# An encoder layer on one core: the first shift-and-scale products run as one block, and one gate step moves ahead of the attention

## The chip, the core and the metric

The kernel runs on one core of a Trainium2 chip. A core has five engines with queues of their own: TensorE (PE in the profile; its weight loads are shown apart as PEld), VectorE (DVE), ScalarE (ACT), GpSimd (POOL) and SyncE (SP). All of SyncE's work here is to issue transfers from device memory to the on-chip memory SBUF. TensorE writes to PSUM, which has eight banks of 128 x 512 fp32 values. The metric is the device time of one execution in microseconds, the median over the runs.

## The reference

One layer of a bidirectional encoder is applied to two groups of 256 rows (prompt and sample) of width 1024, all in fp32:

```python
ada = silu(c) @ w_ada + b_ada
sh1, sc1, g1, sh2, sc2, g2 = split(ada, 6)
h = layernorm(x) * (1 + sc1) + sh1
rq, rk, rv, rg, dq, dkv, kr, gA, gB = split(h @ w_in)
# branch A: two-way retention over 4 heads with rq, rk, rv, gated by silu(rg), times w_ret_o -> y_a
# branch B: cq = rmsnorm(dq), ckv = rmsnorm(dkv); queries cq @ w_uq, keys ckv @ w_uk, values ckv @ w_uv,
#           a shared rotary key from kr; 8 heads of softmax attention, times w_mla_o -> y_b
f = (sigmoid(gA) * y_a + sigmoid(gB) * y_b) @ w_out
x = layernorm(alpha * x + (1 + g1) * f)
h = layernorm(x) * (1 + sc2) + sh2
# conv-gated MLP of width 2816 -> y
x = layernorm(alpha * x + (1 + g2) * y)
```

## The kernel before

The 512 rows of both groups stand side by side as columns: h is kept transposed as eight tiles `hT[k]` of 128 features x 512 rows, k = 0 to 7. Nearly every fp32 product is made of three TensorE matmuls (`mm3`, L161 to L163): each operand is split into a high part (a rounded cast, on ScalarE as a rule, L151) and a low part (the difference, on VectorE, L141), and high x high, high x low and low x high are added up in PSUM. A weight must therefore land, be cast and be subtracted before its second or third matmul can run. In the names `_r` is the raw weight, `_h` and `_l` are the parts.

The start works in four quarters q = 0 to 3, two h tiles each. `ada_sums(q)` (L371) multiplies silu(c) into eight pieces `wada` of 128 x 512, of which each product fills only 32 rows of a PSUM bank; four of them lie beside each other, so that the eight products of a quarter come in two rounds. `ada_rows` (L377) copies the sums to SBUF on ScalarE, `ada_done` turns them (TensorE, `ps_adx`, L384) and reduces them (VectorE, L386) to the shift `sh1` and scale `sc1` of the quarter; `h_tile` applies these to the turned, normalized x (`xT`, made by `flip_x`) and splits h. `latent(k)` adds h tile k times the latent weight `wlat` k (448 columns: dq, dkv, kr) into four banks `ps_lat`, and `gb_part` does the same for the first two tiles of gate B. `keep_warm` (L291) issues matmuls of ones whose result is not used.

Before, quarter 0's products are cut in two: four stand inside the first turned tile, four behind the fourth, and each later quarter's two fours have latent products between them. `lat_hi` casts the first latent weight on ScalarE; its low part (`lat_lo`) is handed to `h_tile` and made on VectorE between the two halves of h tile 0.

After the last latent product come the norms and the latent rows: `latent_rows` turns the latents, scales them and splits them to `cqT0`, `cqT1` and `ckvT`. The rest of gate B and the first piece of gate A lie in a row of steps, `fill_b` (32 steps of six matmuls, 128 x 512). `take(fill_b, cost)` draws steps until the cost is reached, 1.3 for each; ahead of the attention `take(fill_b, 2.6)` draws two. A weight of a gate is loaded and split once for eight steps. The attention (`mla`) is a generator that yields a cost with each piece, and `interleave` draws a gate step whenever the gates' cost falls behind a fixed share, so the places of the steps in the attention are set by costs alone. While a head pair is worked on, the next pair's projections are made: `mla_proj(j)` splits weight `wm` j and makes `qn`, `kn`, `qr` and `v`; `scores` makes `ps_s`, its negative maximum `nm` and the exponentials `p`; `flip` turns `p`.

TensorE's order is the order of the program throughout. ScalarE's and VectorE's orders are that of the program in the start (up to the last `gb_part`), and from there a scheduler of the language sets them at build time. SyncE issues the loads in the order of the program as their buffers come free; raw weights, high parts and low parts have two buffers each.

Of the kernel before, what the change touches and what calls it, by code (L numbers as in the profile page):

```python
# [22 lines left out]

NP = 7

WARM_FIRST, WARM_THEN, WARM_FLIP = 9, 16, {1: 5, 3: 2}
IN_ORDER = {PE, mybir.EngineType.Activation, mybir.EngineType.DVE}

D = 1024
# [2 lines left out]
NK = D // 128  # L32
# [5 lines left out]
LATENT = 448  # L38
# [71 lines left out]
def encoder_kernel(ctx: ExitStack, tc: tile.TileContext, ins, outs):  # L110
# [264 lines left out]
    def ada_rows(q):  # L375
        ada_rows_of[q] = t512(F32, f"row{q}")
        act.copy(ada_rows_of[q], ps_ada.pop(q))  # L377
# [35 lines left out]
    def flip_x(k):  # L413
        ps = ps512(f"ps_xt{k}")
        for t in range(4):
            if k == 0 and t == 2:
                ada_sums(0, range(4))
            elif k == 0 and t:
                keep_warm(WARM_FLIP[t])
            pe.transpose(ps[:, t * 128:(t + 1) * 128], xs[t][k // 4][:, (k % 4) * 128:(k % 4) * 128 + 128], ident)  # L420
        xT[k] = t512(F32, f"xT{k}")
        (dve.tensor_copy if k in (1, 3) else act.copy)(xT[k], ps)
# [6 lines left out]

    lat_parts = {}  # L430

    def lat_hi(k):
        wl = lat_parts[k] = tuple(w[:, :LATENT] for w in (t512(F32R, f"wlat{k}_h"), t512(F32R, f"wlat{k}_l")))
        act.copy(wl[0], lat_raw[k][:, :LATENT])

    def lat_lo(k):
        wl = lat_parts[k]
        sub(wl[1], lat_raw.pop(k)[:, :LATENT], as32(wl[0]))

    def lat_split(k):  # L440
        lat_hi(k)
        lat_lo(k)

    def latent(k, ts=range(4)):
# [33 lines left out]
    def ada_chunk(which, cc):  # L478

        col = which * D + cc * 512  # L480
        acc = [t512(F32, f"acc{which}_{cc}_{g}") for g in range(2)]
        for kq in range(4):
            for k in range(2):
                raw = t512(F32, f"araw{which}_{cc}_{kq}_{k}")
                nc.sync.dma_start(raw, w_ada[:, kq * 2 + k, col:col + 512])
                for g in range(2):
                    s = csil[:, g, kq * 2 + k:kq * 2 + k + 1]
                    if kq == 0 and k == 0:
                        dve.tensor_scalar(out=acc[g], in0=raw, scalar1=s, scalar2=None, op0=ALU.mult)
                    else:  # L490
                        dve.scalar_tensor_tensor(out=acc[g], in0=raw, scalar=s, in1=acc[g],  # L491
                                                 op0=ALU.mult, op1=ALU.add)
            yield 0.0
        parts = [split(acc[g], f"accp{which}_{cc}_{g}") for g in range(2)]
        if which in (2, 5):
            bb = t512(F32, f"bb{which}_{cc}")
            nc.gpsimd.dma_start(bb, ins["b_ada"][:, col:col + 512].to_broadcast([128, 512]))
        yield 0.0
        yield 0.0
        for g in range(2):  # L500
            ps = ps512(f"ps_sum{which}_{cc}_{g}")
            pe.matmul(ps, ones, parts[g][0], start=True, stop=False)
            pe.matmul(ps, ones, parts[g][1], start=False, stop=True)
            full = t512(F32, f"ada{which}_{cc}_{g}")
            if which in (2, 5):
                dve.scalar_tensor_tensor(out=full, in0=ps, scalar=1.0, in1=bb, op0=ALU.add, op1=ALU.add)
                if which == 5:
                    act.mul(full, full, 1.0 / ALPHA)
                gates[which, g, cc] = full
            else:  # L510
                blocks = full.rearrange("p (k f) -> p k f", k=4)
                mul(blocks, ps.rearrange("p (k f) -> p k f", k=4), ident.unsqueeze(1).to_broadcast([128, 4, 128]))
                v = small(4, f"adv{which}_{cc}_{g}")
                dve.reduce_sum(out=v, in_=blocks, axis=AX.X)
                dst, one = (sh2, 0.0) if which == 3 else (sc2, 1.0)
                ks = slice(cc * 4, cc * 4 + 4)
                dve.scalar_tensor_tensor(out=dst[:, ks, g], in0=v, scalar=one, in1=bT[:, which, ks], op0=ALU.add, op1=ALU.add)
        yield 0.86


    with tc.manual_schedule(engines={PE}):
# [67 lines left out]
        with tc.manual_schedule(engines=IN_ORDER - {PE}):  # L589
            start_b()  # L590
            norm_x()
            flip_x(0)
            flip_x(1)
            flip_x(2)
            flip_x(3)
            ada_sums(0, range(4, NK))
            ada_rows(0)
            lat_hi(0)
            ada_done(0)
            h_tile(0, lambda: lat_lo(0))  # L600
            lat_hi(1)
            h_tile(1, lambda: lat_lo(1))
            flip_x(4)
# [1 line left out]
            load_vectors()  # L605
            latent(0, (2, 3, 0, 1))
            latent(1, (2, 3))
            ada_sums(1, range(4))
            latent(1, (0, 1))
            gb_split(0)  # L610
            lat_split(2)
            ada_sums(1, range(4, NK))
            ada_rows(1)
            gb_part(0, (0,))
            for q in range(1, 4):
                if q > 1:
                    latent(2 * q - 2)
                    lat_split(2 * q)
                    ada_sums(q, range(4))
                    latent(2 * q - 1, range(2))  # L620
                    ada_sums(q, range(4, NK))
                    ada_rows(q)
                    latent(2 * q - 1, range(2, 4))
                ada_done(q)
                h_tile(2 * q)
                lat_split(2 * q + 1)
# [61 lines left out]
        act.copy(K2[64:128], ps[0:64])  # L688
        sub(KL[0][0:64], ps[0:64], as32(K2[0:64]))
        act.copy(KL[1][64:128], as32(KL[0][0:64]))  # L690
        take(fill_b, 2.6)


        w_uq = ins["w_uq"][0].rearrange("(k p) (h f) -> p k h f", p=128, f=192)
# [727 lines left out]
```

## Time and profile before

| | us |
|---|---|
| Median of 3 runs (lowest, highest) | 864.46 (864.42, 866.68) |
| The profiled execution | 865.91 |
| Its span, with a granted TensorE clock of 0.997 | 864.1 |
| TensorE busy | 849.4 |
| VectorE busy | 612.1 |
| ScalarE busy | 379.1 |
| GpSimd busy | 95.0 |

The span runs from the first to the last recorded event, and the time of the execution lies 1.8 us above it. The start with its quarters takes the span's first 52 us, norms and latent rows come up to about 76, the attention up to 175, and then come the output of branch B, retention, merge and the MLP. A row of the timeline gives start, duration, engine, line, operation, output<-inputs, and in brackets the engine's idle time ahead of it with what ended it. A TensorE matmul's duration includes the time until its result is out, so consecutive matmuls overlap in these rows, and the distance of their starts is what one costs.

### The profile page before, as it was taken

What the parts mean: (1) busy time and instruction counts of PE and PEld (TensorE: products, weight loads), DVE (VectorE), ACT (ScalarE), POOL (GpSimd) and SP (SyncE); (2) the same over time, 40 slices, a digit from 0 to 9 for tenths busy, and PEclk for the clock granted to TensorE, in tenths of its full rate; (3) what the DMA queues carried; (4) which work ended last, traced back from release to release, by engine and by line L of the source; (5) the groups of instructions that cost most, each with busy time, mean ns of one, the idle gap of its engine ahead of it and who ended that gap; (6) DMA issues with size and microseconds to landing.
All of it is one profiled execution on the core that took longest, in us unless ns stands there. A gap on an engine that the chain in (4) does not pass through costs nothing.

```text
span 864.1 us, 11309 instructions
## 1 busy us (share of the span) xinstructions
PE 849.4 (98%) x4209; PEld 710.7 (82%) x4209; DVE 612.1 (71%) x1052; ACT 379.1 (44%) x647; POOL 95.0 (11%) x141
## 2 busy tenths in 40 slices
PE   8999999999999999999999999999999999999996
PEld 5678888988878888888888899888888888888885
DVE  5465888883687788796977867578657756855666
ACT  3564877551344344354343265334433535443500
POOL 3031012363000101000010200000000000100100
PEclk9999999999999999999999999999999999999998
DMA  9943156799465533553358323255343564655731
GB/s 296 352 151 110 50 154 182 197 295 240 146 179 175 171 114 118 156 181 138 117 159 261 121 87 98 74 157 156 97 138 121 154 176 133 157 166 150 263 115 66
DMA packets 129624, 137.63 MB, mean 159 GB/s; under 512 B 8757, under 2 KB 96403, under 8 KB 129568
## 3 DMA queue, kind: packets, MB, share of 16 engines
q1 hardware_dynamic: 118864, 112.75, 41.8%
q0 software_dynamic: 9888, 23.14, 11.7%
q10 hardware_dynamic: 816, 1.02, 0.3%
q8 instruction: 33, 0.54, 0.2%
q14 instruction: 23, 0.19, 0.1%
HBM read 129.53 MB, written 22.03 MB: 175 GB/s over the span
## 4 chain that ended last, share of the span: by engine, by line
PE 91%; DVE 3%; DMA 2%; ACT 2%; issue 1%; SPq 0%; ACTq 0%; DVEq 0%
PE ps_b L161 5%; PE ps_b L163 5%; PE ps_b L162 5%; PE ps_a L162 5%; PE ps_a L163 5%; PE ps_a L161 5%; PE ps_d L163 4%; PE ps_d L162 4%; PE ps_d L161 4%; PE ps_ga L161 2%; PE ps_ga L162 2%; PE ps_ga L163 2%; PE ps_rg L162 2%; PE ps_rg L163 2%; PE ps_ya L163 2%; PE ps_rg L161 2%
## 5 line engine op out<-in xcount | busy, mean ns | idle before, releaser
L491 DVE SCALAR_TENSOR_TENSOR acc<-araw,csil,acc 128x512 f32<-128x512 f32 x112 | 77.9, 748 | 18.8 <-DMA araw<-in_w_ada_dram 18.8
L161 PE MATMUL ps_b<-h_h,wup_h 128*128 128x512 f32 (+1 forms) x200 | 72.8, 364 | 0.3 <-ACT h2m L401 0.3
L162 PE MATMUL ps_a<-h_l,wup_h 128*128 128x512 f32 (+1 forms) x200 | 72.9, 365 | 0.1
L163 PE MATMUL ps_a<-h_h,wup_l 128*128 128x512 f32 (+1 forms) x200 | 72.8, 364 | 0.0
L161 PE MATMUL ps_a<-h_h,wup_h 128*128 128x512 f32 (+1 forms) x200 | 72.8, 364 | 0.0
L163 PE MATMUL ps_b<-h_h,wup_l 128*128 128x512 f32 (+1 forms) x200 | 72.7, 364 | 0.0
L162 PE MATMUL ps_b<-h_l,wup_h 128*128 128x512 f32 (+1 forms) x200 | 72.7, 364 | 0.0
L141 DVE TENSOR_TENSOR wup_l<-wup_r,wup_h 128x1024 fp32r<-128x1024 f32 (+1 forms) x46 | 52.7, 1173 | 8.4 <-ACT wup_h L151 7.7
L151 ACT CAST wup_h<-wup_r 128x1024 fp32r<-128x1024 f32 (+1 forms) x46 | 44.3, 1013 | 27.8 <-PE ps_b L162 20.0
L144 DVE TENSOR_TENSOR conv<-conv,ps_b 128x512 f32<-128x512 f32 x22 | 15.1, 686 | 40.2 <-PE ps_b L163 36.7
L161 PEld LDWEIGHTS ps_b<-h_h,wup_h 128*128 128x128 f32 x200 | 37.7, 189 | 6.4 <-ACT h2m L401 0.5
L162 PEld LDWEIGHTS ps_a<-h_l,wup_h 128*128 128x128 f32 x200 | 37.7, 189 | 6.3 <-DVE h_l L141 0.3
L163 PEld LDWEIGHTS ps_a<-h_h,wup_l 128*128 128x128 f32 x200 | 37.7, 189 | 6.2 <-DVE wup_l L141 0.2
L162 PEld LDWEIGHTS ps_b<-h_l,wup_h 128*128 128x128 f32 x200 | 37.7, 189 | 6.0
L163 PEld LDWEIGHTS ps_b<-h_h,wup_l 128*128 128x128 f32 x200 | 37.7, 189 | 5.9
L161 PEld LDWEIGHTS ps_a<-h_h,wup_h 128*128 128x128 f32 x200 | 37.7, 189 | 5.8
L1203 ACT ACTIVATE conv<-ps_a,vecs 128x512 f32<-128x512 f32 x22 | 17.2, 780 | 41.7 <-PE ps_a L163 41.7
L1205 DVE SCALAR_TENSOR_TENSOR conv<-ps_a,vecs,conv 128x510 f32<-128x510 f32 x22 | 16.4, 747 | 24.0 <-ACT conv L1203 24.0
L1209 ACT ACTIVATE conv<-conv 128x512 f32<-128x512 f32 x22 | 13.9, 633 | 41.2 <-DVE conv L1207 41.1
L1274 POOL DMA_DIRECT2D x1d<-ux x12 | 10.7, 929 | 175.9 <-DVE ux L144 111.4
L848 POOL DMA_DIRECT2D wsum<-in_w_down_dram x42 | 28.1, 1171 | 7.3 <-DMA wsum<-in_w_down_dram 7.1
L151 ACT CAST w_h<-w_r 128x1024 fp32r<-128x1024 f32 (+1 forms) x20 | 17.9, 944 | 19.2 <-PE ps_d L163 10.2
(383 smaller groups left out, 2461.6 us busy)
## 6 DMA issues: line engine op xcount, KB each, us to landing
wup_r<-in_w_up_dram SPq DMA_DIRECT2D x44, 512.0 KB, 5.3
araw<-in_w_ada_dram SPq DMA_DIRECT2D x64, 256.0 KB, 5.6
wsum<-in_w_down_dram POOLq DMA_DIRECT2D x42, 256.0 KB, 7.7
wada<-in_w_ada_dram SPq DMA_DIRECT2D x32, 256.0 KB, 5.9
w_r<-wsum SPq DMA_DIRECT2D x28, 256.0 KB, 3.8
wga_r<-in_w_in_dram SPq DMA_DIRECT2D x4, 1024.0 KB, 5.4
wmo_r<-in_w_mla_o_dram SPq DMA_DIRECT2D x4, 1024.0 KB, 5.3
wqk_r<-in_w_in_dram SPq DMA_DIRECT2D x8, 512.0 KB, 5.5
```

Source lines behind the costliest of these rows:

```text
L141: return (eng or dve).tensor_tensor(out=out, in0=a, in1=b, op=ALU.subtract)
L144: (eng or dve).tensor_tensor(out=out, in0=a, in1=b, op=ALU.mult)
L151: last_split.append(act.copy(hi, src).ins)
L161: pe.matmul(out, l[0], r[0], start=start, stop=False, skip_group_check=skip)
L162: pe.matmul(out, l[0], r[1], start=False, stop=False, skip_group_check=skip)
L163: pe.matmul(out, l[1], r[0], start=False, stop=stop, skip_group_check=skip)
L491: dve.scalar_tensor_tensor(out=acc[g], in0=raw, scalar=s, in1=acc[g], op0=ALU.mult, op1=ALU.add)
L848: tc.keep_in_program_order(nc.gpsimd.dma_start(dst, src, **kw))
L1203: act.activation(a, pa, AF.Identity, scale=convw[:, 1, f:f + 1], bias=convb[:, f:f + 1])
L1205: dve.scalar_tensor_tensor(out=av_[:, :, 1:256], in0=pv[:, :, 0:255], scalar=convw[:, 0, f:f + 1], in1=av_[:, :, 1:256], op0=ALU.mult, op1 ...
L1209: act.activation(a, a, AF.Gelu)
L1274: nc.gpsimd.dma_start(x1_rows(t, c), u, accum_op=ALU.add)
```

## The change

In quarter 0 all eight shift-and-scale products now stand together behind the second turned tile, the third and fourth tile are turned behind them, and matmuls of ones stand at the place of the four that left (`WARM_FLIP` has 3 for the place t = 2). The first latent weight is split whole ahead of the sums' copy, with the cast on VectorE in place of ScalarE. In each later quarter the eight products stand together: in quarter 1 behind all latent products, in quarters 2 and 3 behind one row tile's latent products of the odd h tile. One more gate step is drawn ahead of the attention (3.9 in place of 2.6, three steps). The edit in `ada_chunk` only writes the same two matmuls as a loop.

```diff
-WARM_FIRST, WARM_THEN, WARM_FLIP = 9, 16, {1: 5, 3: 2}
+WARM_FIRST, WARM_THEN, WARM_FLIP = 9, 16, {1: 5, 2: 3, 3: 2}
...
     def flip_x(k):
         ps = ps512(f"ps_xt{k}")
         for t in range(4):
-            if k == 0 and t == 2:
-                ada_sums(0, range(4))
-            elif k == 0 and t:
+            if k == 0 and t:
                 keep_warm(WARM_FLIP[t])
...
-    def lat_hi(k):
+    def lat_hi(k, eng=None):
         wl = lat_parts[k] = tuple(w[:, :LATENT] for w in (t512(F32R, f"wlat{k}_h"), t512(F32R, f"wlat{k}_l")))
-        act.copy(wl[0], lat_raw[k][:, :LATENT])
+        (eng.tensor_copy if eng else act.copy)(wl[0], lat_raw[k][:, :LATENT])
...
-    def lat_split(k):
-        lat_hi(k)
+    def lat_split(k, eng=None):
+        lat_hi(k, eng)
         lat_lo(k)
...
             flip_x(0)
             flip_x(1)
+            ada_sums(0)
+            lat_split(0, dve)
+            ada_rows(0)
             flip_x(2)
             flip_x(3)
-            ada_sums(0, range(4, NK))
-            ada_rows(0)
-            lat_hi(0)
             ada_done(0)
-            h_tile(0, lambda: lat_lo(0))
+            h_tile(0)
...
             latent(1, (2, 3))
-            ada_sums(1, range(4))
             latent(1, (0, 1))
             gb_split(0)
             lat_split(2)
-            ada_sums(1, range(4, NK))
+            ada_sums(1)
             ada_rows(1)
...
                     lat_split(2 * q)
-                    ada_sums(q, range(4))
-                    latent(2 * q - 1, range(2))
-                    ada_sums(q, range(4, NK))
+                    latent(2 * q - 1, range(1))
+                    ada_sums(q)
                     ada_rows(q)
-                    latent(2 * q - 1, range(2, 4))
+                    latent(2 * q - 1, range(1, 4))
...
-        take(fill_b, 2.6)
+        take(fill_b, 3.9)
```

Three places show how instructions move. The first is VectorE's queue at the start, before: `xT` are copies of turned tiles, `adv0` the reduction for shift and scale of quarter 0, `h0_l` and `wlat0_l` low parts.

```order
L422 COPY xT1_329<-ps_xt1_324 128x512
L422 COPY xT3_343<-ps_xt3_338 128x512
L386 TENSOR_REDUCE adv0_359<-ps_adx0_354 128x8
L147 TENSOR_TENSOR sh1_236<-adv0_359,bT_197 128x4
L389 SCALAR_TENSOR_TENSOR sc1_237<-adv0_359,bT_197 128x4
L405 TENSOR_SCALAR hm0_1_365<-xT0_322,sc1_237,sh1_236 128x256
L141 TENSOR_TENSOR h0_l_364<-hm0_1_365,h0_h_363 128x256
L141 TENSOR_TENSOR wlat0_l_352<-wlat0_115,wlat0_h_351 128x448
```

The same queue with the change:

```order
L420 COPY xT1_327<-ps_xt1_322 128x512
L432 CAST wlat0_h_338<-wlat0_115 128x448
L141 TENSOR_TENSOR wlat0_l_339<-wlat0_115,wlat0_h_338 128x448
L420 COPY xT3_356<-ps_xt3_351 128x512
L386 TENSOR_REDUCE adv0_363<-ps_adx0_358 128x8
L147 TENSOR_TENSOR sh1_236<-adv0_363,bT_197 128x4
```

The first latent weight's cast, new on this engine, and its low part now stand ahead of the copy of the fourth tile, and so ahead of the reduction.

The second place is TensorE in quarter 2, before, from the last latent product of h tile 2 on (h tiles 2 and 3 are worked on while the shifts of quarter 2 are summed).

```order
L163 MATMUL ps_lat3_241<-wlat2_h_440,h2_l_463 128x448
L371 MATMUL ps_ada2_525<-wada2_0_146,c32_195 32x512
L371 MATMUL ps_ada2_525<-wada2_1_148,c32_195 32x512
L371 MATMUL ps_ada2_525<-wada2_2_150,c32_195 32x512
L371 MATMUL ps_ada2_525<-wada2_3_152,c32_195 32x512
L161 MATMUL ps_lat0_238<-wlat3_h_472,h3_h_476 128x448
...
L163 MATMUL ps_lat1_239<-wlat3_h_472,h3_l_477 128x448
L371 MATMUL ps_ada2_525<-wada2_4_154,c32_195 32x512
```

With the change:

```order
L163 MATMUL ps_lat0_238<-wlat3_h_475,h3_l_480 128x448
L371 MATMUL ps_ada2_531<-wada2_0_146,c32_195 32x512
L371 MATMUL ps_ada2_531<-wada2_1_148,c32_195 32x512
L371 MATMUL ps_ada2_531<-wada2_2_150,c32_195 32x512
L371 MATMUL ps_ada2_531<-wada2_3_152,c32_195 32x512
L371 MATMUL ps_ada2_531<-wada2_4_154,c32_195 32x512
L371 MATMUL ps_ada2_531<-wada2_5_156,c32_195 32x512
L371 MATMUL ps_ada2_531<-wada2_6_158,c32_195 32x512
L371 MATMUL ps_ada2_531<-wada2_7_160,c32_195 32x512
L161 MATMUL ps_lat1_239<-wlat3_h_475,h3_h_479 128x448
```

The two fours have become one block, one latent group (three matmuls) later than the first four stood and one group earlier than the last four.

The third place is VectorE in the attention, about the second head pair's projections (`qn1_1`, `kn1_1`, `v1_0`, `v1_1`), the next pair's weight `wm2` and the fourth gate weight `wgb3`. Before:

```order
L141 TENSOR_TENSOR qn1_1_l_1191<-ps_qn1_1_1183,qn1_1_h_1190 128x512
L769 TENSOR_REDUCE nm1_0_1230<-ps_s1_0_1219 128x2
L141 TENSOR_TENSOR kn1_1_l_1199<-ps_kn1_1_1194,kn1_1_h_1198 128x512
L141 TENSOR_TENSOR v1_0_l_1210<-ps_v1_0_1202,v1_0_h_1209 128x512
L141 TENSOR_TENSOR wm2_l_1330<-wm2_r_1322,wm2_h_1329 128x640 x2
L776 RECIPROCAL r1_0_1236<-sm1_0_1233 128x2
L769 TENSOR_REDUCE nm1_1_1271<-ps_s1_1_1260 128x2
L141 TENSOR_TENSOR v1_1_l_1248<-ps_v1_1_1240,v1_1_h_1247 128x512
L778 TENSOR_SCALAR p1_0_1232<-p1_0_1232,r1_0_1236 128x256 x2
L141 TENSOR_TENSOR wgb3_l_1351<-wgb3_r_1348,wgb3_h_1350 128x1024 x2
```

With the change:

```order
L141 TENSOR_TENSOR qn1_1_l_1200<-ps_qn1_1_1192,qn1_1_h_1199 128x512
L765 TENSOR_REDUCE nm1_0_1239<-ps_s1_0_1228 128x2
L141 TENSOR_TENSOR wgb3_l_1295<-wgb3_r_1292,wgb3_h_1294 128x1024 x2
L141 TENSOR_TENSOR kn1_1_l_1208<-ps_kn1_1_1203,kn1_1_h_1207 128x512
L141 TENSOR_TENSOR wm2_l_1350<-wm2_r_1342,wm2_h_1349 128x640 x2
L141 TENSOR_TENSOR v1_0_l_1219<-ps_v1_0_1211,v1_0_h_1218 128x512
L772 RECIPROCAL r1_0_1245<-sm1_0_1242 128x2
L765 TENSOR_REDUCE nm1_1_1280<-ps_s1_1_1269 128x2
L141 TENSOR_TENSOR v1_1_l_1257<-ps_v1_1_1249,v1_1_h_1256 128x512
```

The split of `wgb3`, which stood behind all of these, now stands ahead of `kn1_1_l`, and that of `wm2` ahead of `v1_0_l`. ScalarE's casts of the same four moved in the same way.

More of the change, by code (lines that the diff above doesn't have):

```diff
@@ L501, in ada_chunk @@
             ps = ps512(f"ps_sum{which}_{cc}_{g}")
-            pe.matmul(ps, ones, parts[g][0], start=True, stop=False)
-            pe.matmul(ps, ones, parts[g][1], start=False, stop=True)
+            for part in parts[g]:
+                pe.matmul(ps, ones, part, start=part is parts[g][0], stop=part is parts[g][1])
             full = t512(F32, f"ada{which}_{cc}_{g}")
```

## The prediction

> **What bounds the kernel now.** I read the chain of waits first, then the busy time by stage, then the start and the attention as a timeline.
>
> ```profile
> span 864.1 us, 11309 instructions
> PE 91%; DVE 3%; DMA 2%; ACT 2%; issue 1%; SPq 0%; ACTq 0%; DVEq 0%
> ...
> 18.30:22.30 4.00, 2.32 (x18) 1.53 (x14) 1.91 (x7) 2.72 (x6) 0.00 (x0) 1.00 1.10 348
> ...
> 22.30:51.80 29.50, 29.50 (x164) 20.23 (x164) 14.14 (x33) 14.32 (x27) 4.50 (x3) 1.00 1.02 332
> ...
> 88.20:175.10 86.90, 86.56 (x550) 77.56 (x549) 71.94 (x143) 63.48 (x147) 18.50 (x32) 1.00 0.56 155
> 175.10:864.10 689.00, 679.71 (x3247) 571.50 (x3246) 489.39 (x779) 271.69 (x415) 58.21 (x80) 1.00 0.52 152
> ```
>
> The columns of the stage rows are length, then busy time of PE, PEld, DVE, ACT and POOL with counts, granted clock, DMA share and GB/s. TensorE carries 91% of the chain and is busy for 86.56 of 86.90 us in the attention (88.2 to 175.1): what is won before it arrives at the end unless the attention gives some back. After 175.1 the change alters no tensor work, so I let the gain or loss at 175 stand for the whole. Only small gaps can be won. The matmuls between 22.3 and 51.8 show as busy throughout, yet a matmul's shown time includes its drain, so I read start times there, not busy time. The DMA engines are full until 51.8 (share 1.0 to 1.1), so landings there depend on bytes queued, not on what TensorE does.
>
> **The start (take −0.56).** The gap ends in the latent products.
>
> ```profile
> 17.50 1.07 PE L371 MATMUL ps_ada<-wada,c 128*32 128x512 f32 x8
> ...
> 19.84 1.04 PE L420 MATMUL ps_xt<-cst,x 128*128 128x128 f32 x8
> 20.04 0.19 DVE L386 TENSOR_REDUCE adv<-ps_adx 128x8 f32<-128x32 f32 x1 [1.74 <-PE ps_adx L384]
> ...
> 21.25 0.47 PE L161 MATMUL ps_lat<-wlat_h,h_h 128*128 128x448 f32 x1 [0.38 <-ACT h_h L404]
> 21.57 0.62 DVE L141 TENSOR_TENSOR wlat_l<-wlat,wlat_h 128x448 fp32r<-128x448 f32 x1
> 22.25 0.48 PE L162 MATMUL ps_lat<-wlat_l,h_h 128*128 128x448 f32 x1 [0.52 <-DVE wlat_l L141]
> 22.56 0.36 PE L163 MATMUL ps_lat<-wlat_h,h_l 128*128 128x448 f32 x1
> ...
> 23.48 0.62 DVE L141 TENSOR_TENSOR wlat_l<-wlat,wlat_h 128x448 fp32r<-128x448 f32 x1
> ...
> 25.65 0.37 PE L163 MATMUL ps_lat<-wlat_h,h_l 128*128 128x448 f32 x1
> ```
> ```profile
> 10.65 1.05 SPq L229 DMA_DIRECT2D wada<-in_w_ada_dram  x2
> ...
> wada<-in_w_ada_dram SPq DMA_DIRECT2D x2, 256.0 KB, 5.9
> ...
> 24.58 7.19 SPq L229 DMA_DIRECT2D wada<-in_w_ada_dram  x8
> ...
> wada<-in_w_ada_dram SPq DMA_DIRECT2D x2, 256.0 KB, 5.8
> ```
>
> The second latent matmul waits for the low part of the first latent weight: 22.25 where a follower comes 0.31 after its predecessor (22.25 to 22.56, with an exposed weight load). From the third (22.56) to the eighteenth (25.65) are 15 steps of 0.206. Without the wait the third would start at 21.25+0.31+0.21 = 21.77 instead of 22.56: 0.79. The change makes that low part on VectorE before the shift and scale are ready. Its new cast waits there for the weight: the last shift-and-scale piece of quarter 0 is issued at 11.70−0.37 = 11.33 and lands 5.9 later, at 17.2; the latent weight is next in the same queue and lands within the next microsecond, by 18.0 (my estimate from 256 KB pieces at 349 GB/s). Cast and subtraction, 0.62 each at most, end by about 19.2.
>
> The eight shift-and-scale products now run in one run from about 15.35 and cannot end before the piece of 17.2. Four products take 1.07 us; what is left for the last piece ends near 18.3, against 17.50+1.07 = 18.57 before. But two transposed tiles (8 transposes, 1 us by the row of 19.84) now stand behind them, ahead of the row's turning, and VectorE copies one of them (about 0.7, as its work on 128x512 out of PSUM takes below) ahead of the reduction: about 19.2+0.05+0.7 = 20.0 against the reduction's 20.04. The first latent matmul therefore stays at 21.25; I cost the re-ordering itself at nothing, with −0.2 to +0.6 as bounds (the upper one if cast and subtraction run 0.6 later than said and hold the copy up).
>
> Part of the 0.79 returns. The next latent weight's low part is still made at 23.48 to 24.10, behind h on VectorE, and the fourteenth matmul, which needs it, would now come at 21.77+11×0.206 = 24.04. With 0.06 for the release (21.57+0.62 to 22.25) and an exposed load of 0.1 that costs up to 0.23. So −0.79+0.23 = **−0.56**, between 0 and −0.79.
>
> **Eight products together (take −0.28, −0.10, −0.28).**
>
> ```profile
> 25.94 1.06 PE L371 MATMUL ps_ada<-wada,c 128*32 128x512 f32 x8
> 26.94 0.47 PE L161 MATMUL ps_lat<-wlat_h,h_h 128*128 128x448 f32 x1
> 27.25 0.36 PE L162 MATMUL ps_lat<-wlat_l,h_h 128*128 128x448 f32 x1
> ...
> L371 PE MATMUL ps_ada<-wada,c x48: 592/605/617, 12.7 to 39.1; 128*32 128x512 f32 x48
> ...
> 35.89 0.37 PE L163 MATMUL ps_lat<-wlat_h,h_l 128*128 128x448 f32 x1
> ```
>
> A group of four starts 25.94−(25.65+0.206) = 0.085 late, holds the next load for 1.00 (26.94) and leaves a slow first follower (0.31 where 0.206 is usual: 0.10). Inside, 1.06 less one matmul's 0.605 is 0.455: two passes of that, and 0.09 until the load. Two groups cost 2×(0.085+0.91+0.09+0.10) = 2.37; eight together 0.085+1.82+0.09+0.10 = 2.10. Saved: about **0.28** in each of three quarters, bounds 0 and −0.35.
>
> Quarter 2 gives some back. Its last piece is issued at 24.58+7.19−0.37 = 31.40 and lands 5.8 later, at 37.2. The gain so far (0.84) puts the end of the first four latents at 35.89+0.21−0.84 = 35.26, three more take 0.62, and the eight begin at 35.96. The fifth to eighth piece are wanted after two passes, at 36.87, so the eighth is 0.35 late. What of this reaches the end depends on how the last passes overlap: 0 to 0.35, I take 0.18. In quarters 1 and 3 I assume all pieces have landed.
>
> **One more gate step before the attention (take −0.76).**
>
> ```profile
> 76.40 0.39 PE L161 MATMUL ps_qn<-cqT_h,wm_h 128*128 128x512 f32 x1
> ...
> 77.09 0.40 PE L161 MATMUL ps_qn<-cqT_h,wm_h 128*128 128x512 f32 x1
> 77.24 0.69 DVE L141 TENSOR_TENSOR cqT_l<-cqT_f,cqT_h 128x512 fp32r<-128x512 f32 x1
> ...
> 77.98 0.50 PE L162 MATMUL ps_qn<-cqT_l,wm_h 128*128 128x512 f32 x1 [0.49 <-DVE cqT_l L141]
> 78.31 0.39 PE L163 MATMUL ps_qn<-cqT_h,wm_l 128*128 128x512 f32 x1
> ```
>
> Three matmuls take 77.09−76.40 = 0.69, or 0.23 each. The one due at 77.32 starts at 77.98 (0.66), and its follower comes 0.33 later instead of 0.23: 0.76. A gate step is six such matmuls, 1.38, and now stands ahead of these; the same work falls out later, so it costs nothing by itself. At the new place cqT_l (77.93) is wanted at 78.70: the whole **0.76** goes, bounds −0.6 and −0.8.
>
> **What the step moves in the attention (take +1.06).** Gates are computed in a fixed row of steps; one taken early brings each later gate weight's split one slot forward. The split of the fourth gate weight thereby comes, on ScalarE and VectorE, ahead of three splits that the attention needs at once.
>
> ```profile
> 103.78 0.68 DVE L769 TENSOR_REDUCE nm<-ps_s 128x2 f32<-128x512 f32 x1
> 104.38 0.68 DVE L141 TENSOR_TENSOR kn_l<-ps_kn,kn_h 128x512 fp32r<-128x512 f32 x1
> 104.97 0.69 DVE L141 TENSOR_TENSOR v_l<-ps_v,v_h 128x512 fp32r<-128x512 f32 x1
> 105.57 1.55 DVE L141 TENSOR_TENSOR wm_l<-wm_r,wm_h 128x640 fp32r<-128x640 f32 x2
> ...
> 108.82 2.36 DVE L141 TENSOR_TENSOR wgb_l<-wgb_r,wgb_h 128x1024 fp32r<-128x1024 f32 x2
> 111.09 0.70 DVE L141 TENSOR_TENSOR pT_l<-ps_pt,pT_h 128x512 fp32r<-128x512 f32 x1
> ...
> 102.78 0.61 ACT L151 CAST kn_h<-ps_kn 128x512 fp32r<-128x512 f32 x1
> ...
> 106.76 2.00 ACT L151 CAST wgb_h<-wgb_r 128x1024 fp32r<-128x1024 f32 x2
> ...
> 108.41 0.40 PE L161 MATMUL ps_qn<-cqT_h,wm_h 128*128 128x512 f32 x1
> ```
>
> In before, the second head's kn_l and v_l come straight behind nm, then wm_l, and wgb_l long after. In the change nm is followed by wgb_l, kn_l, wm_l, v_l. Starts on VectorE lie closer than the shown times: 0.59 behind 0.68 (104.38 to 104.97), 2.27 behind 2.36 (108.82 to 111.09), so about 1.47 behind 1.55. On before's axis: wgb_l at 104.38 (its casts, 2.00 us on ScalarE, take the place of kn_h at 102.78 and end at 104.8, ahead of its second half's start at about 105.5), kn_l at 106.65, wm_l at 107.25, v_l at 108.72, done at 109.41. The next head's qn matmuls, which by the program wait for that v_l to free their bank, cannot start before 109.47. Before they start at 108.41: **+1.06**. The earlier wait for kn_l and scores is inside this. Bounds: 0, if the bank is free earlier than I read, and +1.39 with full times in a row (103.78+0.68+2.36+0.68+1.55+0.69 = 109.74). I take 1.06, since these rows show the overlap.
>
> **Sum.** −0.56−0.28−0.10−0.28−0.76+1.06 = −0.92. The profiled execution took 865.91 with a span of 864.1; it becomes 864.99. It lies 1.45 over the median of the runs, 864.46, which moves by the same amount, to **863.5**. A difference below 0.3% (2.6 us, to 861.87 or 867.05) can hardly be told from none.
>
> **Rivals.**
> First, no wait in the attention: other banks come round, or TensorE has slack there that I missed. For it: in the stage 88.2 to 175.1 TensorE is short of busy by only 0.34, so before all splits came in time. Against it: VectorE is busy 71.94 of 86.90, and 2.27 of work enters ahead of an operand. Then −1.98: 862.5.
>
> Second, slower: the moved splits hold VectorE up twice, in full. At the fourth gate weight 1.39, and one slot early again at the first of the other gate's weights, whose split of the same shape (2.36) then stands ahead of the reduction for a softmax. Together 3.75, more than the 1.98 won elsewhere, from which point it decides: +1.8, 866.2. Against it: there only the reduction is passed, and a split's own halves leave room.
>
> Third, the start brings nothing: VectorE's early cast waits for its weight and delays the copy, reduction and h by 0.6, which eats the 0.56; TensorE then comes late enough in quarter 2 to find its last piece landed. Then 0−0.28×3−0.76+1.06 = −0.54: 863.9. For it: the bound of +0.6 above. Against it: the landing of the latent weight by 18.0 leaves cast and subtraction the time in which TensorE transposes.
>
> Fourth, the clock falls. From 15.3 on TensorE now has eight products, of which the last wait for their pieces until 17.2, and then a thinly filled stretch until 21.25.
>
> ```profile
> 1.48 4.21 PE L291 MATMUL ps_warm<-ones 128*128 128x512 f32 x9 [1.48 <-DVE ones L276]
> ```
>
> A cold start shows its price: nine matmuls in 4.21, 0.47 each against 0.23 at speed, so about 2.1 lost. Net −0.92+2.1 = +1.2: 865.6. Against it: granted clock is 1.00 between 18.3 and 22.3, where TensorE is busy 2.32 of 4.00. The Trainium skill (TensorE: Matmul & The Clock Gate, section "What's actually happening") says that an idle window of about 3.4 us halves the clock. By that rule the gaps here, each under 2 us, would not close it, and the row of 18.3 to 22.3 agrees.
>
> **How the numbers follow.** The forecast gets 0.50, the first rival 0.20, the second 0.12, the third 0.12, the fourth 0.06. The forecast's own bounds are 863.1 (0.23 and 0.18 not given back: −1.33) to 864.4 (nothing from the start, 1.39 in the attention: −0.92+0.56+0.33 = −0.03). The range 862.2 to 865.1 takes in the first and third rival, and of the second as much as half of its second place (1.39+1.18−1.98 = +0.6); it leaves out the rest of the second and the fourth. Only the second or fourth with more on top passes 867.05, and only more gain than any term shows passes 861.87: faster 0.06, same 0.89, slower 0.05.
>
> **What would show it.** Right: first latent near 21.2 and the second 0.31 behind it; one run of eight products per quarter, with no latent between them; in quarter 2 a DMA wait inside the group; no wait for cqT_l; in the attention TensorE waits near 105 to 108 (on the new axis) for kn_l and v_l, with wgb_l ahead of both. Wrong: the first latent later than 21.5, TensorE waits anywhere after 110, or a granted clock under 1 at 18 to 22. A total gain near 2 us would say that the attention's queue did not matter; a loss, that it mattered twice.

## The result and the profile after

The change made the kernel slower: 870.86 us in the median (869.38 to 872.24), against 865.33 for the kernel before (864.42 to 870.2) in 11 runs each. The ratio is 1.0054, with an interval of 1.004 to 1.0068. The forecast was 863.5. The profiled execution of the change took 869.88 with a span of 868.1, which is 4.0 over the 864.1 of before.

The chain of waits of the change, and its busy time by stage, on the stages that were shown of before (but the first begins at 17.50 in place of 18.30, and the last ends at the new span):

```profile
PE 91%; DMA 3%; DVE 3%; ACT 1%; issue 1%; SPq 0%; DVEq 0%; ACTq 0%
...
17.50:22.30 4.80, 4.27 (x29) 3.36 (x28) 3.39 (x10) 3.21 (x7) 0.00 (x0) 1.00 1.10 349
22.30:51.80 29.50, 29.50 (x169) 21.33 (x168) 15.04 (x37) 15.16 (x29) 4.75 (x3) 1.00 1.01 331
...
88.20:175.10 86.90, 86.25 (x542) 76.87 (x541) 72.07 (x142) 64.55 (x148) 19.29 (x33) 1.00 0.53 137
175.10:868.10 693.00, 678.58 (x3238) 571.10 (x3236) 487.15 (x777) 268.21 (x412) 55.99 (x78) 0.99 0.52 153
```

The last stage is 4.0 longer than before while TensorE's busy time in it is 1.1 shorter: the loss is idle time behind 175.1, in the stage that the prediction took as untouched. Between 170 and 260 the waits of TensorE name one place:

```profile
PE ps_yb L163 <- DVE wmo_l L141: 5.3, 1, 5.3
```

`ps_yb` is branch B's output, with four weights `wmo0` to `wmo3` in turn; each is loaded, cast and subtracted like the others. The timeline of the change around that wait, TensorE first, then VectorE, then SyncE:

```profile
194.94 0.39 PE L162 MATMUL ps_yb<-attn_l,wmo_h 128*128 128x512 f32 x1
200.66 0.80 PE L163 MATMUL ps_yb<-attn_h,wmo_l 128*128 128x512 f32 x1 [5.33 <-DVE wmo_l L141]
201.25 0.63 PE L161 MATMUL ps_yb<-attn_h,wmo_h 128*128 128x512 f32 x1
...
203.69 0.40 PE L161 MATMUL ps_yb<-attn_h,wmo_h 128*128 128x512 f32 x1
...
194.74 1.41 DVE L489 SCALAR_TENSOR_TENSOR acc<-araw,csil,acc 128x512 f32<-128x512 f32 x2 [15.38 <-DMA araw<-in_w_ada_dram]
...
199.39 1.22 DVE L141 TENSOR_TENSOR wmo_l<-wmo_r,wmo_h 128x1024 fp32r<-128x1024 f32 x1
...
164.26 0.34 SPq L483 DMA_DIRECT2D araw<-in_w_ada_dram  x1
174.94 0.37 SPq L192 DMA_DIRECT2D wmo_r<-in_w_mla_o_dram  x1
175.36 11.52 SPq L483 DMA_DIRECT2D araw<-in_w_ada_dram  x7
...
DMA to landing us min/median/max: 5.9/20.2/21.5
```

The last row is from the view of the `araw` tiles between 160 and 200. The same two queues before:

```profile
165.10 4.79 SPq L485 DMA_DIRECT2D araw<-in_w_ada_dram  x8
178.61 0.38 SPq L192 DMA_DIRECT2D wmo_r<-in_w_mla_o_dram  x1
...
DMA to landing us min/median/max: 6.8/7.3/7.6
```

`araw` are pieces of the weight for the second layer half's shift, scale and gates; VectorE multiplies them by silu(c) and adds them up (`ada_chunk`), in a long side work that only fills gaps. Before, all eight pieces of the first chunk were issued from 165.10 on, landed in 7 us, and the load of `wmo3` came behind them at 178.61. In the change the order that is made at build time puts the load of `wmo3` ahead of seven of them. (Unlike what the description of the kernel says, SyncE's order too is made at build time: in the program four of these pieces stand ahead of the load of `wmo1`, while in the trace of before the loads of `wmo1` and `wmo2` come ahead of all eight, at 145.32 and 153.32.) That load waits for a raw buffer, which comes free when `wmo1` is subtracted, at 174.9; SyncE issues in order, so the seven pieces left from 175.36 on, over 11.5 us, and took 20 us in the median. VectorE also works in order: it stood 15.38 us in front of the late piece, with the low part of `wmo2` behind it. TensorE lost 200.66−194.94−0.23 = 5.5 there. Then the seven intervals to 203.69 took 3.03 where seven at 0.23 take 1.6: 1.4 more.

How far the change was ahead (−) or behind at one and the same matmul is read from the two timelines. Each row is one execution. The first column is that execution's own start. It ranges over 2.2 us, and the latest starts are those in which the matmuls of ones at the beginning ran slowly:

```profile
7.52 3.92 PE L291 MATMUL ps_warm<-ones 128*128 128x512 f32 x16
7.49 6.71 PE L295 MATMUL ps_warm<-ones 128*128 128x512 f32 x16
```

The first row is of before, the second of skip_slot5_sum_later: there twelve of the fifteen distances between starts are 0.43 us, where in before all but the first are 0.23 or 0.24. Eight of the 13 traces, but not those of before and the change, have six or more distances of 0.43.

| Start in the kernel's trace minus that of before, us | first latent (21.25) | last latent (60.79) | first ps_yb (175.16) | last ps_yb (219.40) | last ps_rg (367.29) |
|---|---|---|---|---|---|
| the change | −0.37 | −2.03 | −2.23 | +4.74 | +3.87 |
| two_steps | −0.45 | −1.53 | −1.54 | −1.54 | +0.19 |
| step_alone | +1.34 | +1.28 | +1.06 | +8.67 | +7.66 |
| load_behind | −0.80 | −1.81 | −1.98 | −1.95 | +1.14 |
| third_raw_buffer | −0.82 | −2.29 | −2.48 | +13.66 | +12.66 |
| wmo2_low_on_gpsimd | −0.54 | −2.21 | −2.40 | −2.11 | +1.54 |
| start_alone | −0.42 | −1.02 | −1.04 | −1.04 | −2.04 |
| two_steps_sum_later | −0.50 | −2.17 | −2.17 | −2.17 | −2.49 |
| load_behind_sum_later | +0.12 | −1.52 | −1.69 | −1.66 | −1.90 |
| skip_slot5 | −0.26 | −1.88 | −2.10 | −2.10 | −2.47 |
| skip_slot5_sum_later | +0.86 | −0.81 | −1.03 | −1.03 | +0.75 |
| skip_slot6_sum_later | +0.37 | −1.29 | −1.50 | −1.50 | −2.13 |

From 367 to the end no kernel's shift changes by more than 0.15. The kernel before ran from 863.7 to 872.4 over all the runs here, so the ratios, each against runs of before on the same chip, have wide intervals, and the traces carry more than they do.

### The profile page after: what moved, and what is told of

Same layout as the page of the kernel before. It is cut to its first block, busy times and chain, and to the rows that moved or that the text cites. A ratio compares the mean times of both kernels' runs of the same rounds, so it can differ in the third digit from the quotient of the medians.

```text
span 868.1 us, 11318 instructions
## 1 busy us (share of the span) xinstructions
PE 849.6 (98%) x4212; PEld 713.2 (82%) x4212; DVE 612.3 (71%) x1053; ACT 378.1 (44%) x646; POOL 93.6 (11%) x141
## 3 DMA queue, kind: packets, MB, share of 16 engines
q10 hardware_dynamic: 816, 1.02, 0.3%
## 4 chain that ended last, share of the span: by engine, by line
PE 91%; DMA 3%; DVE 3%; ACT 1%; issue 1%; SPq 0%; DVEq 0%; ACTq 0%
PE ps_b L161 5%; PE ps_b L162 5%; PE ps_b L163 5%; PE ps_a L162 5%; PE ps_a L163 5%; PE ps_a L161 5%; PE ps_d L162 4%; PE ps_d L161 4%; PE ps_d L163 4%; DMA araw<-in_w_ada_dram 2%; PE ps_ga L161 2%; PE ps_ga L162 2%; PE ps_rqk L161 2%; PE ps_rg L161 2%; PE ps_rqk L162 2%; PE ps_rv L161 2%
## 5 line engine op out<-in xcount | busy, mean ns | idle before, releaser
L163 PE MATMUL ps_yb<-attn_h,wmo_l 128*128 128x512 f32 x64 | 25.7, 401 | 5.3 <-DVE wmo_l L141 5.3
```

The costliest lines, as they stand in the source:

```text
L163: pe.matmul(out, l[1], r[0], start=False, stop=stop, skip_group_check=skip)
```

## The experiments

### Which part of the change does it: two_steps, step_alone

The first undoes one part, the second does it alone on the kernel before.

```diff
 two_steps (on the change)
-        take(fill_b, 3.9)
+        take(fill_b, 2.6)
 step_alone (on the kernel before)
-        take(fill_b, 2.6)
+        take(fill_b, 3.9)
```

> The change with two gate steps ahead of the attention, as before, and the rest of the change kept. Theory A: the loss comes from the third gate step alone. It shifts the build-time order so that the load of the last output weight of branch B (wmo3) stands ahead of seven araw loads and holds them; VectorE then waits for araw with wmo2's low part behind it. Without the step that order is as before: no wait of TensorE for wmo_l, cqT_l waited for again (about 0.7), span about 2.0 under before (862.1, from the shift of 2.0 that the change shows at the end of quarter 3). Theory B: the loss comes from reaching the output of branch B earlier, when its weights have not landed; then at least 2 of the 5.3 us of waiting remain and the span is 864 or more.

> The kernel before with three gate steps in place of two and nothing else. Theory A: the same late araw loads and a wait of TensorE for wmo_l of 4 to 6 us; the time some 5 us over before (won 0.8 at cqT_l, 0.6 behind it, lost 1.2 in the attention, 6.9 at the output of branch B, 0.9 regained behind it). Theory B: TensorE gets there at before's time within 1 us, so no such wait, and the time is within 1 us of before.

Measured: two_steps 864.66 (ratio 0.999, interval 0.9972 to 1.0009, span 864.3); step_alone 871.87 (ratio 1.007, 1.0044 to 1.0096, span 871.7). In two_steps the wait at `ps_yb` is gone, and 1.54 of lead stands at 219.40. In step_alone it is there, with none of the new start. TensorE's wait and SyncE's queue in step_alone:

```profile
PE ps_yb L163 <- DVE wmo_l L141: 5.6, 1, 5.6
...
167.55 0.34 SPq L485 DMA_DIRECT2D araw<-in_w_ada_dram  x1
178.24 0.37 SPq L192 DMA_DIRECT2D wmo_r<-in_w_mla_o_dram  x1
178.66 11.73 SPq L485 DMA_DIRECT2D araw<-in_w_ada_dram  x7
```

So the gate step alone makes the late loads, and Theory B (coming too early) falls: step_alone reached branch B's output 1.06 later than before and still waited. But two_steps did not keep its lead: span 864.3 where 862.1 was expected. It lost 1.7 at another place, between 219 and 254:

```profile
252.60 0.50 PE L501 MATMUL ps_sum<-accp_h,ones 128*128 128x512 f32 x1 [1.71 <-ACT accp_h L151]
```

These matmuls sum the second chunk of the side work. Before, they start at 252.41, so their operand came 0.2 later although all ahead of them was 1.5 sooner.

### Is it SyncE's order: load_behind, third_raw_buffer

```diff
 load_behind (on the change)
-        for dst, src in pieces(raw):
-            nc.sync.dma_start(dst, src)
+        with tc.issue_after(last_piece[0]) if name == "wmo3" else nullcontext():
+            for dst, src in pieces(raw):
+                nc.sync.dma_start(dst, src)
...
+                if which == 4 and cc == 0:
+                    last_piece[:] = [d.ins]
 third_raw_buffer (on the change)
-    T_BUFS = 72
+    T_BUFS = 68
-        raw = wpool.tile([128, 2048], F32, tag="raw", name=name + "_r", bufs=2)
+        raw = wpool.tile([128, 2048], F32, tag="raw", name=name + "_r", bufs=3)
```

> The change with one edit: the load of wmo3 is kept behind the last of the eight araw loads in SyncE's queue. Theory A: araw lands in about 7 us as before, no wait for wmo_l; the shift of the change at the start of branch B's output (0.85 us ahead of before, with the gate step counted) stands to the end: span 863.0 to 863.5. Theory B: a wait of several us stays, since the weights themselves are what is late; span over 866.

> The change with three buffers for raw weights in place of two (four of the 72 general tiles given up for it). The load of wmo3 stands ahead of all araw loads in SyncE's queue but waits for no buffer any more. Theory A1: the harm of the order is that SyncE stands still until wmo1's buffer comes free; then araw is issued near 165, lands within about 10 us, and TensorE waits less than 1 us for wmo_l: span 863 to 865. Theory A2: the harm is that 1 MB goes ahead of araw in the transfer; then araw lands 10 us or more later than in before and the wait for wmo_l stays at 3 us or more.

Measured: load_behind 864.92 (ratio 0.999, 0.9967 to 1.0013, span 865.2). SyncE's queue is as before again, and there is no wait at `ps_yb`:

```profile
164.52 4.62 SPq L484 DMA_DIRECT2D araw<-in_w_ada_dram  x8
175.20 0.38 SPq L193 DMA_DIRECT2D wmo_r<-in_w_mla_o_dram  x1
```

Its lead of 1.95 at 219.40 is kept through branch B's output, which settles Theory A; the expected 0.85 was too small, because it took the extra gate step off a second time at a point where both kernels have done all steps. The span missed its expectation for the reason that two_steps had shown: 2.0 us of waiting for accp_h at 252.49, and a low clock behind it (last section).

Third_raw_buffer came out at 879.03 (ratio 1.0122, 1.0086 to 1.0159) and answered another question than was asked. With a third buffer the load of `wmo3` no longer waited, but in the order made at build time the next two raw loads (`wqk`) stood at its place, and these waited. (The edit also takes four of the 72 general tiles, which could change that order by itself.) Its SyncE queue, VectorE's idle time and TensorE's wait:

```profile
174.70 1.26 SPq L192 DMA_DIRECT2D wqk_r<-in_w_in_dram  x2
176.01 19.36 SPq L483 DMA_DIRECT2D araw<-in_w_ada_dram  x7
...
203.21 3.40 DVE L489 SCALAR_TENSOR_TENSOR acc<-araw,csil,acc 128x512 f32<-128x512 f32 x5 [24.10 <-DMA araw<-in_w_ada_dram]
...
PE ps_yb L163 <- DVE wmo_l L141: 14.0, 1, 14.0
```

The same mechanism, larger. A1 and A2 are not told apart by it, so how much of the harm is SyncE standing still and how much the bytes ahead stays open.

### Is it VectorE's order: wmo2_low_on_gpsimd

```diff
-                wc = k_cols(w_mla_o, 0, NK, j * 256, 256, f"wmo{j}")
+                wc = k_cols(w_mla_o, 0, NK, j * 256, 256, f"wmo{j}", lo_eng=pool if j == 2 else None)
```

> The change, with the low part of wmo2 made on GpSimd in place of VectorE; SyncE's order, with the load of wmo3 ahead of seven araw loads, stays. Theory A: araw lands as late as in the change (VectorE waits 15 us for it) but holds only what stands behind it on VectorE; wmo2's low part does not, so TensorE waits under 1 us for wmo_l unless GpSimd comes to it late, and the shift of about -0.9 is kept to the end of branch B's output (before: 219.4). Rival: the late loads hold TensorE in another way, too (the weights wmo2 or wmo3 themselves late); then 3 us or more of waiting stay.

Measured: 867.82 (ratio 1.0025, 1.0005 to 1.0045, span 865.6). SyncE's queue is as bad as in the change, and VectorE still stands for `araw`; GpSimd makes the low part meanwhile:

```profile
164.09 0.34 SPq L483 DMA_DIRECT2D araw<-in_w_ada_dram  x1
174.77 0.37 SPq L192 DMA_DIRECT2D wmo_r<-in_w_mla_o_dram  x1
175.19 10.52 SPq L483 DMA_DIRECT2D araw<-in_w_ada_dram  x7
...
190.49 4.52 DVE L489 SCALAR_TENSOR_TENSOR acc<-araw,csil,acc 128x512 f32<-128x512 f32 x4 [11.31 <-DMA araw<-in_w_ada_dram]
...
184.78 2.40 POOL L141 TENSOR_TENSOR wmo_l<-wmo_r,wmo_h 128x1024 fp32r<-128x1024 f32 x1 [3.62 <-ACT wmo_h L151]
```

No wait for wmo_l is left, and the lead at 219.40 is 2.11 (the expected 0.9 came from the same slip as in load_behind). Up to there the late side loads cost TensorE nothing, once nothing that it needed stood behind them in VectorE's queue. At 252.34 this kernel, too, waited 2.03 for accp_h.

### The lead that ends at 252, and the later sum

One edit, on three kernels: the matmuls of that sum come one step later, with the next chunk's first loads where they were.

```diff
+        if (which, cc) == (4, 1):
+            yield 0.0
         for g in range(2):
             ps = ps512(f"ps_sum{which}_{cc}_{g}")
...
-        yield 0.86
+        if (which, cc) != (4, 1):
+            yield 0.86
```

> The change with two gate steps, and the matmuls that sum the second shift chunk (ps_sum of chunk 4,1) one step later in TensorE's order, every load where it was. With two gate steps TensorE came 1.55 us ahead of before to these matmuls and waited there 1.7 us for accp_h and then 0.2 for accp_l, which came at 252.6 as in before (252.4). Theory W: that operand's time is set by a chain of loads and not by TensorE, so whatever is won earlier ends there; with the matmuls 5 us later no such wait, and the shift of 1.55 stands to the end: span 862.3 to 862.8. Rival: TensorE waits for another late load of the same chain instead (wqk, wrg) and the span stays within 0.5 of 864.3.

> The change with both edits: the load of wmo3 behind the araw loads and the later sum. By Theory A and Theory W together neither the 5.3 us at wmo_l nor the 2.0 us at accp_h: the shift at the end of branch B's output (-1.95 in the run with the first edit alone) stands to the end, span 861.5 to 862.5, and the time is below before by 1.5 to 3. If only one of the theories holds, 864 or more.

Measured: two_steps_sum_later 863.51 (ratio 0.9968, 0.9948 to 0.9988, span 861.5), load_behind_sum_later 863.9 (ratio 0.9984, 0.9975 to 0.9993, span 862.2). In both the sum finds its operands at once, here in two_steps_sum_later, and the lead at 219.40 is not lost behind it:

```profile
255.54 0.40 PE L503 MATMUL ps_sum<-accp_h,ones 128*128 128x512 f32 x1
```

The expected 1.55 became 2.17 mostly because that profile also lacks a late piece that two_steps had in quarter 2 (below).

That the edit ended the wait is not shown by these two profiles. ScalarE's casts to accp_h, in two_steps, two_steps_sum_later and (with the fifth place of the attention empty, next section) skip_slot5_sum_later:

```profile
251.93 1.34 ACT L151 CAST accp_h<-acc 128x512 fp32r<-128x512 f32 x2 [8.56 <-DVE acc L489]
248.88 1.34 ACT L151 CAST accp_h<-acc 128x512 fp32r<-128x512 f32 x2 [7.42 <-DVE acc L489]
252.98 1.35 ACT L155 CAST accp_h<-acc 128x512 fp32r<-128x512 f32 x2 [8.56 <-DVE acc L493]
```

In two_steps_sum_later the first of the two casts was done at 249.51, so the sum would not have waited at its old place either, which TensorE reached at about 250.1 (252.27 in before, less 2.17); load_behind_sum_later has 249.44 against 250.6. And start_alone and skip_slot5, without the later sum, have 250.13 and 249.88 and did not wait at accp_h. In all 13 traces but third_raw_buffer the first cast is done 9.9 to 10.0 us after the last load of its chunk is issued, and those loads came between 239.5 and 243.7 in the kernels that are ahead at 219.40, whether their lead was large or small. So the operand does come by a chain of loads, as Theory W says, but it is late in some executions and not in others. What makes these loads early or late is open. Only in skip_slot5_sum_later was the operand late (253.60) where the sum had been moved: there the sum stands at 256.68 and did not wait. The times of the runs speak for the edit, too: above 866 us lie 12 of the 36 runs of two_steps, load_behind and skip_slot5, and 2 of the 35 of the same three with the later sum, on other chips.

### The gate step's place in the attention: skip_slot5, skip_slot6, and the sum

The extra step stays ahead of the attention, and one place inside it is left empty, so that all later gate work stands where it was.

```diff
-def interleave(main, filler, ratio):
+def interleave(main, filler, ratio, skip=0):
...
+            draws += 1
+            if draws == skip:
+                done += 1.3
+                continue
...
-        interleave(mla(), fill_b, FILL_MLA)
+        interleave(mla(), fill_b, FILL_MLA, skip=5)
```

> The change, but the fifth gate step inside the attention is left out of its place, so that from there on every gate weight is split where it was before, and one gate step stands directly ahead of branch B's output again. Theory A with the attention's queue loss as told: neither the 1.2 us in the attention nor the wait for wmo_l appear; span 860.7 to 861.5 (shift of 3.4 at 90 us kept). Rival: the place without a gate step lacks cover for the softmax or the splits there and TensorE waits up to 1.4 us: 862 to 862.5. If the loss has nothing to do with the gate step's place: 868.

> The kernel with the fifth place in the attention left empty, and the same later sum. In its profile that sum was in time, so by Theory W the profile stays at 861.6 within 0.5, and the runs of it at 867 to 869 become fewer if those are runs in which that operand was late. Rival: the spread has another cause; then the highest runs stay at 867 or more.

> As the kernel with the fifth place left empty and the later sum, but the sixth place is empty. The wait of 0.6 us for wgb_l at 108 in that kernel came from the fifth; with the sixth the splits stand one place further from it: shift at branch B's output 0.3 to 0.8 better relative to the start of the latents, span 860.8 to 862 at an ordinary start. Rival: the wait only moves, and it is equal to the fifth within 0.3.

Measured: skip_slot5 863.5 (ratio 0.9989, 0.9967 to 1.0011, span 861.6), with the later sum 864.05 (0.9957, 0.9937 to 0.9976, span 864.9), skip_slot6 with the later sum 863.85 (0.9971, 0.9954 to 0.9987, span 862.1). The wait for kn_l in the attention and the wait at `ps_yb` are both gone, but the emptied place makes one of its own, the same with the fifth (108.05) as with the sixth, shown here:

```profile
108.66 0.50 PE L167 MATMUL ps_gb<-h_h,wgb_l 128*128 128x512 f32 x1 [0.57 <-DVE wgb_l L145]
```

So the lead at 175 is about that of the change (−1.84 against −1.86 when the first column is taken off) and not the 3.4 that was expected: taking the waits out at one place gave them back at the next. For the sixth place a gain of 0.3 to 0.8 was expected; the lead at 175, without the first column, is 1.87 against 1.84, so its rival (the wait only moves) held. The expectation of 3.4 had also read the lead at 90 us in a place where the kernels stand one gate step apart.

The expectation for skip_slot5_sum_later failed in the profile: it lost 1.8 at the next sum of the same chain, 43 us on. VectorE had waited 1.0 for a load of that sum (291.68), and made its low parts behind the split of `wqk`:

```profile
295.71 0.49 PE L507 MATMUL ps_sum<-accp_h,ones 128*128 128x512 f32 x1 [0.89 <-ACT accp_h L155]
297.44 0.50 PE L507 MATMUL ps_sum<-accp_l,ones 128*128 128x512 f32 x1 [1.23 <-DVE accp_l L145]
```

That profile is of the slowest of its runs. Its runs did lie closer (862.96 to 866.69 against 862.58 to 868.83 without the later sum), but the later sum moves the meeting with that chain rather than ending it.

### What the start gives: start_alone

Only quarter 0's new order, with the later quarters and the gate steps as before:

```diff
 (on the change)
-                    latent(2 * q - 1, range(1))
-                    ada_sums(q)
+                    ada_sums(q, range(4))
+                    latent(2 * q - 1, range(2))
+                    ada_sums(q, range(4, NK))
                     ada_rows(q)
-                    latent(2 * q - 1, range(1, 4))
+                    latent(2 * q - 1, range(2, 4))
...
-        take(fill_b, 3.9)
+        take(fill_b, 2.6)
```

> Quarter 0's new order alone: the later quarters' products in fours and two gate steps as before. By the change's trace the start brings 0.9 to 1.1 at the end of quarter 1's latents against before, and each later quarter's block of eight 0.36. So here the shift is 0.8 to 1.1 from there to the attention, against 1.5 with all three blocks. Rival: the blocks of eight bring nothing by themselves and the shift is 1.5.

Measured: 868.47 (863.93 to 871.6; ratio of the comparison 1.001, 0.9985 to 1.0034), span 862.2. The lead is 1.03 at the first gate product, 0.42 of it the execution's own start, and 1.02 at the last latent, as expected. The blocks of eight therefore add what the change has beyond it. The trace is of the fastest of its ten runs, 4.5 under their median, and what the slower runs lost no trace here shows. In the change and in two_steps the block of quarter 2 reads:

```profile
35.49 1.92 PE L371 MATMUL ps_ada<-wada,c 128*32 128x512 f32 x16
...
35.47 2.42 PE L371 MATMUL ps_ada<-wada,c 128*32 128x512 f32 x16
```

The first is an undisturbed block; in two_steps a late piece held it by 0.50. Of the ten traces with this block three were held: this one, load_behind (by 0.64) and third_raw_buffer (by 0.12).

## Why the prediction was wrong

By 175.1 it was right in sign and too cautious; its sum failed at the sentence that nothing behind 175.1 is touched. Its own sign of being wrong, a wait of TensorE after 110, is what came.

- **The start, −0.56.** The change went from −0.37 at the first latent to −1.17 at the third, and to −0.94 behind the second latent weight's wait: 0.80 won and 0.23 returned, as told. Whether the re-ordering itself moved the first latent is not shown: the kernels with the new order range from −0.82 to +0.86 there.
- **Eight together, −0.28, −0.10, −0.28.** Measured −0.36 in each of the three quarters of the change. The late piece that was told for quarter 2 did not come in it, and where it came (0.50, 0.64 and 0.12) it did not cost the 0.18 of the sum.
- **One more gate step, −0.76.** Measured −0.77 (−0.68 at 76.40 to −1.45 at 78.31). A further −0.6 came by 90, which had no term: the lead grows there in the first scores (88.75) and about the next qn (89.83), where before waits 0.2 for the high part of the weight.
- **The attention, +1.06.** Measured +1.19, from −2.04 at the matmul of 90.17 in before to −0.85 at that of 108.65. VectorE's queue stood as told:

```profile
101.73 0.68 DVE L765 TENSOR_REDUCE nm<-ps_s 128x2 f32<-128x512 f32 x1
102.33 2.35 DVE L141 TENSOR_TENSOR wgb_l<-wgb_r,wgb_h 128x1024 fp32r<-128x1024 f32 x2
104.59 0.68 DVE L141 TENSOR_TENSOR kn_l<-ps_kn,kn_h 128x512 fp32r<-128x512 f32 x1
105.20 1.55 DVE L141 TENSOR_TENSOR wm_l<-wm_r,wm_h 128x640 fp32r<-128x640 f32 x2
106.66 0.69 DVE L141 TENSOR_TENSOR v_l<-ps_v,v_h 128x512 fp32r<-128x512 f32 x1
...
105.33 0.66 PE L783 MATMUL ps_pt<-cst,p 128*128 128x128 f32 x4 [0.40 <-DVE kn_l L141]
...
107.49 0.47 PE L161 MATMUL ps_qn<-cqT_h,wm_h 128*128 128x512 f32 x1
```

  About half of the loss, 0.56, came at the turning of `p`, which waits for kn_l; the rest came by the qn. That v_l holds this qn is not shown: v_l was done at 107.35, and the profile puts the weight load of the qn (107.46) behind the last scores, not behind v_l.
- **The sum at 175.** −0.92 was told, −2.23 measured, of which 0.37 is the execution's start: −1.86.
- **The step that failed:** "After 175.1 the change alters no tensor work, so I let the gain or loss at 175 stand for the whole." TensorE's work was unchanged, but VectorE's and SyncE's orders there are made at build time and had changed with the gate step. That cost 6.97 (−2.23 to +4.74), more than all the rest together. Behind it 0.87 came back at 252 and 253, where the operands of the sum hold before up and the late change finds them done. The rival on the slower side had the right kind, an in-order queue with a needed split behind late work, and the wrong place; it looked at split against split in the attention, where the cost was a load against a load on SyncE, with VectorE's queue behind it.
- **The second premise in the same sentence** fails by itself: even where nothing is lost at `ps_yb`, 1.7 to 3.7 of lead ended at 252 in three traces (two_steps, load_behind, wmo2_low_on_gpsimd), because the side work's operands came by a chain of loads that was late there. In start_alone and skip_slot5 it was in time, and their leads grew.
- **The clock rival** had the right kind and the wrong place: in the change the clock fell behind the 5.3 us of waiting (below) and cost 1.4, where 2.1 had been put down for the start. The granted clock of 1.00, which the prediction held against it, need not show the start's clock: it also reads 1.00 in step_alone from 9.0 to 13.3, where the matmuls of ones lie 0.43 apart. In the change all but the first of these come 0.23 apart and the latent matmuls 0.21, so its start was at speed; in eight other traces the matmuls of ones were slow at first.

## What to carry to other kernels

Where a scheduler sets the order of queues, moving one block of matmuls moves loads and vector work far behind it: compare the order on every queue to the end of the program, and for each load that has moved ask what it waits for and which loads now stand behind it. A wait for a buffer on an in-order load queue passes to whatever comes next, and from there through an in-order vector queue to an operand that has nothing to do with it. A lead at one point counts only as far as the next place where the time is set by loads; of the versions here only the four with the later sum have intervals wholly below 1: 0.9957 and 0.9971 with the fifth and the sixth place empty, 0.9968 with two gate steps, 0.9984 with the load of `wmo3` behind. Their intervals overlap, and those of the same kernels without the later sum (0.9989, 0.999 and 0.999) overlap with them, so no best one is shown.

## What the runs showed of the hardware that was not expected

After the 5.3 us in which TensorE waited, its clock was low for 3 us. The stages of the change around the wait, with the granted clock in the third column from the right:

```profile
190.00:195.10 5.10, 5.10 (x24) 4.09 (x22) 0.36 (x1) 0.41 (x1) 2.38 (x4) 1.00 1.07 353
195.10:200.60 5.50, 0.23 (x2) 0.00 (x0) 4.94 (x8) 1.58 (x2) 1.34 (x3) 0.95 1.11 261
200.60:203.70 3.10, 3.04 (x8) 2.41 (x9) 3.10 (x6) 0.00 (x0) 0.00 (x0) 0.53 1.05 391
203.70:210.00 6.30, 6.30 (x29) 5.24 (x28) 6.30 (x11) 1.25 (x2) 0.00 (x0) 1.00 0.79 234
```

A granted clock of 0.53 for 3.1 us made a wait of 5.5 cost 6.97. A much shorter wait did the same in load_behind, at the sum at 252:

```profile
250.40:252.50 2.10, 0.09 (x2) 0.01 (x1) 2.10 (x6) 0.62 (x1) 0.00 (x0) 1.00 0.30 54
252.50:254.70 2.20, 2.10 (x5) 1.33 (x6) 2.17 (x6) 2.13 (x5) 0.01 (x1) 0.55 1.07 371
```

Its 2.0 us of waiting (2.02) cost 3.1 with the low clock (−1.95 to +1.14), and in wmo2_low_on_gpsimd a wait of 2.03 there was followed by a granted clock of 0.53 from 254.0 to 256.7 (3.65 lost), while the 1.7 us of two_steps at the same matmul were followed by a granted clock of 1.00 (1.73 lost). The Trainium skill (TensorE: Matmul & The Clock Gate, section "What's actually happening") has the clock halved after an idle window of about 3.4 us. The half agrees with 0.53 and 0.55; the length does not, since waits of 2.0 us were enough here, and so the prediction's comfort that gaps under 2 us are safe rested on a narrow margin. The loads of 256 KB took 20 us in the median when issued between 175 and 187, against 7.3 when issued between 165 and 170 before; the `wsum` traffic of GpSimd's queue and the 1 MB of `wmo3` share the DMA engines in that stretch, and no run here parts the two.
